# A two-block transformer kernel on one core: inputs laid out for the first stage, weight slabs split in two steps, eight buffers for convolution taps

## The chip, the core and the metric

The kernel runs on one core of a Trainium2 chip. Times are device microseconds of one execution. Engines: PE (TensorE) multiplies matrices, DVE (VectorE) and ACT (ScalarE) work elementwise, POOL (GpSimd) does elementwise work beside them, and SP's queue issues most of the loads. Everything is float32 in memory; the large matrix products run on float32r operands.

## The reference, cut to what matters

Two transformer blocks over 512 positions of 1024 channels, batch 1. The first stage, where most of the change lies, computes this:

```
cond  = silu(c) @ ada_w + ada_b            # six vectors of 1024
h     = rmsnorm(x, norm1_g) * (1 + scale1) + shift1
z     = h @ w_in + b_in                    # u, v, val, gate: 512 columns each
y_a   = gelu(u) * (causal w_s applied to layernorm(gelu(v)) in chunks of 128 positions)
y     = val * sigmoid(gate)
y_b   = silu(groupnorm(causal depthwise convolution of y, width 31))
x     = x + gate1 * (concat(rmsnorm(y_a), rmsnorm(y_b)) @ w_out)
```

A gated feed-forward layer, a final modulated norm, and a second block (two kinds of attention, two feed-forward layers, a pooling mixer) follow. Their program text is not touched.

## The kernel before, in words

Activations lie with channels on the 128 partitions: X holds eight tiles of 128 channels by 512 positions, two to a buffer. A product keeps float32 accuracy by splitting each operand into a high and a low part: `wh`, `wl` for weights, two halves of `H` for activations, and three matmuls for each pair (wh by high, wh by low, wl by high).

Weights come in slabs of 128 by 1024 elements (512 KB) in the order of a list. `Weights.load` (lines 296 to 318) starts a slab's load on SP's queue; the closure `split` (line 312) copies it to `wh` on ACT and subtracts to get `wl` on DVE. `take` hands out the oldest split slab and then splits further ones until `look` (4) are ready, so both halves of a split stand at the same place of the program. The slabs of `w_in` and `w_out` carry a raised priority (`HP`, line 50).

Which engine runs which instruction when is set by a scheduler at build time that goes by priorities and its own estimates, except where `ordered(True)` (lines 557 to 851) pins the order on DVE, ACT and PE to that of the program. Buffers are recycled by tag; "ar" tiles of 4 KB a partition hold slabs, adaptive-norm weights and most other large tiles.

The first stage goes as follows (lines 232 to 851). Small vectors are loaded as rows and turned by PE (`load_vecs`, `turn`). x arrives by positions, four loads; ACT sums its squares, PE turns it by 32 transposes, and DVE copies the result to X. The weights of shift1 and scale1 arrive as sixteen loads of 512 KB; one `piece(q)` takes four of them, computes 256 columns of each vector in sixteen float32 matmuls on four column groups of PE, adds up the groups, and gives `front(q)` what it needs to make two tiles of H. `products(q)` then multiplies these two tiles with the first four slabs of `w_in`, 24 matmuls into four PSUM banks ("wave"), which stay open over q = 0 to 3. In each q but the last, the next piece's matmuls are put after 6 products (`WV`), its transposes after 4 more (`WT`).

After the wave, `glu_out` makes the convolution's input, and `conv` puts 31 taps for each of four channel tiles into two work lists: the first `nd` (23, then 17) taps run on DVE as one multiply-add each into PSUM, the rest as a scaled copy on ACT into a `tap` buffer (line 748, two buffers) and an add on POOL. `pump` deals these lists out between the products of the other twelve slabs of `w_in` and the first of `w_out`. `center` needs both sums complete. The causal spatial weights are loaded as `wsr`, masked on POOL, turned by eight PE transposes (lines 904 to 908) and copied to `wsT` by ACT.

The functions that the diff touches and their callers:

Of the kernel before, what the change touches and what calls it, by code (L numbers as in the profile page):

```python
# [9 lines left out]
F32 = mybir.dt.float32  # L10
# [15 lines left out]
WV = (6, 0)  # L26
WT = 4
DEEP = 2
# [55 lines left out]

TAGS = {}
TAGSETS = 0
B1 = ("cv", "glu", "bvs", "wsr", "wsT", "vt", "uT")
NB1 = 11
# [32 lines left out]
def body(ctx: ExitStack, tc: tile.TileContext, I: dict, out, dbg=None):  # L121
# [7 lines left out]
    V, G, SC, TE = (Ordered(tc, e) for e in (nc.vector, nc.gpsimd, nc.scalar, nc.tensor))  # L129
# [78 lines left out]
    def flat(apx):  # L208
        n = len(apx.shape)
        letters = "abcde"[:n]  # L210
        return apx.rearrange(f"{' '.join(letters)} -> ({' '.join(letters)})") if n > 1 else apx

    def load_vecs(gi, grp, eng=nc.sync):

        rt = rows.rearrange("p a (s c) -> p (a s) c", c=P)[:, gi]
        r0 = 0
        for name, src, n in grp:
            eng.dma_start(rt[r0:r0 + n, :P], flat(src).rearrange("(r p) -> r p", p=P))
            r0 += n

        def turn():
            pt = ST()
            TE.transpose(pt[:, :r0], rt[:r0, :P], ident[:r0, :r0])
            col = C(r0)
            V.tensor_copy(col, pt[:, :r0])
            c0 = 0
            for name, src, n in grp:
                vecs[name] = col[:, c0:c0 + n]
                c0 += n
        return turn  # L230

    rows = A("rows")
    turn_c = load_vecs(0, [("c", I["c"], 8)])
    xt = []
    for i in range(4):
        a = A("xtok")
        nc.sync.dma_start(a, I["x"][0, i * P:(i + 1) * P, :].rearrange("p (j c) -> p j c", j=2))
        xt.append(a)
    turn_1 = load_vecs(1, [("norm1", I["norm1_g"], 8), ("adab", I["ada_b"], 48), ("b_in", I["b_in"], 16)], nc.scalar)
# [36 lines left out]
    Xp = [cp.tile([P, 2, S], F32, name=f"X{q}") for q in range(4)]  # L276

    def x_(k, c0=0, c1=S):
        return Xp[k // 2][:, k % 2, c0:c1]

# [3 lines left out]
    class Weights:  # L284


        def __init__(self, look):
            self.look, self.deep = look, 1
            self.specs, self.loaded, self.ready, self.done = [], [], [], 0
            self.pool = False  # L290
            self.hp = 0
# [4 lines left out]
        def load(self):  # L296
            parts, kt, ncols, pool, hp = self.specs[self.done]
            n = kt * ncols

            def fl(t):  # L300
                return t.rearrange("p a c -> p (a c)")[:, :n]

            def v(t):
                return fl(t).rearrange("p (k m) -> p k m", k=kt)

            raw = ar.tile([P, 2, S], F32, tag="raw", name="raw", bufs=NR) if NR else A("raw")
            for (p0, p1, c0, c1, src, *ks) in parts:
                k0, k1 = ks or (0, kt)
                nc.sync.dma_start(v(raw)[p0:p1, k0:k1, c0:c1], src)
# [8 lines left out]
            self.loaded.append(split)  # L318

        def _emit(self):  # L320
            while len(self.loaded) < self.deep and self.done < len(self.specs):
                self.load()
            self.loaded.pop(0)()
# [228 lines left out]
    turn_2 = load_vecs(2, [("cw", I["b_conv_w"], 124)])  # L552
    turn_3 = load_vecs(3, [("norm2", I["norm2_g"], 8), ("normf", I["norm_f_g"], 8), ("conv_b", I["b_conv_b"], 4), ("gn_g", I["b_gn_g"], 4),
                           ("gn_b", I["b_gn_b"], 4), ("ona", I["out_norm_a_g"], 4), ("onb", I["out_norm_b_g"], 4), ("lng", I["a_ln_g"], 4),
                           ("lnb", I["a_ln_b"], 4), ("psc", I["pool_scale_2"], 8), ("adafb", I["ada_f_b"], 16), ("pe", I["nsa_cmp_pe_2"], 32)])

    ordered(True)
    turn_c()
    act(cact, vecs["c"], AF.Silu)
    V.tensor_copy(c32, cact.unsqueeze(2).to_broadcast([P, KD, 32]))  # L560
    ssx = C(8).rearrange("p (a b) -> p a b", a=4)
    rsc = C(4)
    for i in range(4):
        for j in range(2):
            act(SQ(), xt[i][:, j], AF.Square, accum_out=ssx[:, i, j:j + 1])
    V.tensor_reduce(rsc, ssx, axis=AX.X, op=OP.add)
    act(rsc, rsc, AF.Sqrt, scale=1.0 / D, bias=epsc)
    V.reciprocal(rsc, rsc)
    for k in range(KD):
        pt = AXP()  # L570
        for i in range(4):
            TE.transpose(pt[:, i * P:(i + 1) * P], xt[i][:, k // 4, (k % 4) * P:(k % 4 + 1) * P], ident)
        V.tensor_copy(x_(k), pt)
    rsx = ACC()
    act(rsx, spread(rsc, S), AF.Copy)
    W.ahead(2)
    turn_1()
    adab = vecs["adab"]

    def piece(q):  # L580

        g = [ada_cols(adaw[q][x], 8 * x + 2 * q, adab[:, 8 * x + 2 * q:8 * x + 2 * q + 2], AXP) for x in range(2)]
        for x in g:
            for _ in range(8):
                yield next(x)
        for x in g:
            yield from x
# [128 lines left out]
    def conv(cs, c0, c1, nd):  # L716
# [119 lines left out]
    for q in range(4):  # L836
        w = products(q)
        if q < 3:
            pc = piece(q + 1)
            for n in WV:  # L840
                for _ in range(n):
                    next(w)
                for _ in range(8):
                    next(pc)
# [8 lines left out]
    turn_2()  # L853
    turn_3()
# [49 lines left out]
    for b in range(2):  # L904
        pt = ST()
        for h in range(4):
            TE.transpose(pt[:, h * P:(h + 1) * P], wsr[:, b, h * P:(h + 1) * P], ident)
        act(wsT[:, b], pt, AF.Copy)
    turn_4()
# [324 lines left out]
    W.deep = DEEPF  # L1234
    f1 = Ffn(HO)
# [553 lines left out]

# [16 lines left out]
```

## Time and profile before

| | us |
|---|---|
| median of 3 runs | 1663.76 |
| lowest and highest run | 1662.12, 1664.29 |
| the profiled execution | 1662.05 |
| its span, first to last instruction | 1660.3 |
| PE busy in it | 1626.7 (98%) |
| DVE busy | 879.6 (53%) |
| ACT busy | 681.0 (41%) |
| POOL busy | 129.3 (8%) |

Busy time of PE is a union of overlapping matmuls, so a busy PE may still run slowly, at half clock for instance. All matmuls of the program carry the line of one helper, L113, so tiles tell them apart: `mm` is a product's bank, `ax` and `st` are other banks, `xtok` is x by positions, `adaw` are weights of the adaptive norm, `fixed` are small vectors.

### The profile page before, as it was taken

To read this page: it belongs to the slowest core of one execution; us is meant where nothing else is said; L and a number is where in the kernel's file an instruction comes from. 1 tells how busy PE (TensorE), PEld (TensorE's weight loads), DVE (VectorE), ACT (ScalarE), POOL (GpSimd) and SP (SyncE) were. 2 spreads that over 40 slices of the span, in tenths; PEclk is the share of its full clock that TensorE was granted. 3 is DMA by queue.
4 is the path that set the end of the run, shared out by engine and by line. 5 is a ranking of instruction groups with operands and counts; after the bars stand their busy time and mean duration, and the time that the engine had idled before them with its cause. 6 is when DMAs were issued, how large, how long until landed. Compare 5 with 4: busy or idle time off the path is not lost.

```text
span 1660.3 us, 21934 instructions
## 1 busy us (share of the span) xinstructions
PE 1626.7 (98%) x8733; PEld 1355.0 (82%) x8733; DVE 879.6 (53%) x1644; ACT 681.0 (41%) x1231; POOL 129.3 (8%) x144
## 2 busy tenths in 40 slices
PE   7998999999999999999999999999998999999998
PEld 5886698888888998777778888888888998888886
DVE  4799583444433584778857344423257734432244
ACT  4585352322123455455658223313237823322232
POOL 0452000000000011101011000000022100000002
PEclk9999999999999999999999999999999999999999
DMA  9635434445452333301144133234221533232511
GB/s 306 180 113 209 161 99 117 136 132 173 146 139 80 95 79 79 90 26 52 39 134 108 51 101 89 83 107 140 77 89 54 138 89 102 75 108 92 144 38 51
DMA packets 245167, 179.53 MB, mean 108 GB/s; under 512 B 20688, under 2 KB 220224, under 8 KB 245064
## 3 DMA queue, kind: packets, MB, share of 16 engines
q1 hardware_dynamic: 240520, 176.99, 36.2%
q10 hardware_dynamic: 4544, 1.14, 0.4%
q8 instruction: 68, 1.11, 0.3%
q14 instruction: 35, 0.29, 0.1%
HBM read 175.99 MB, written 2.11 MB: 107 GB/s over the span
## 4 chain that ended last, share of the span: by engine, by line
PE 86%; DVE 4%; ACT 1%; issue 0%; DMA 0%; DVEq 0%; ACTq 0%
PE mm L113 80%; PE ax L113 3%; PE st L113 3%; DVE pw L113 1%; ACT sq L113 0%; DMA raw<-in_ffn_w_gate_dram 0%; DVE wl L113 0%; ACT pw L113 0%; DVE XT L113 0%; DVE H L113 0%; DVE sq L113 0%; DVE mg L113 0%; DVE pt L113 0%; DVE lg L113 0%; DVE fk L113 0%
## 5 line engine op out<-in xcount | busy, mean ns | idle before, releaser
L113 PE MATMUL mm<-H,wh 128*128 128x512 f32 (+1 forms) x3168 | 869.8, 360 | 7.4 <-ACT H L113 2.4
L113 PEld LDWEIGHTS mm<-H,wh 128*128 128x128 f32 x3168 | 563.7, 189 | 106.6 <-issue 8.7
L113 PE MATMUL mm<-H,wl 128*128 128x512 f32 (+1 forms) x1584 | 567.9, 359 | 0.0
L113 DVE TENSOR_TENSOR wl<-raw,wh 128x1024 fp32r<-128x1024 f32 (+1 forms) x257 | 309.7, 1218 | 232.9 <-ACT wh L113 219.8
L113 PEld LDWEIGHTS mm<-H,wl 128*128 128x128 f32 x1584 | 299.3, 189 | 46.8 <-issue 3.4
L113 ACT ACTIVATE wh<-raw 128x1024 fp32r<-128x1024 f32 (+1 forms) x257 | 261.4, 1040 | 132.6 <-PE mm L113 66.6
L113 PE MATMUL mm<-wh,hid 128*128 128x512 f32 x704 | 217.4, 389 | 0.0
L113 DVE TENSOR_TENSOR silu<-silu,mm 128x512 f32<-128x512 f32 (+1 forms) x77 | 47.0, 611 | 252.2 <-PE mm L113 248.2
L113 PEld LDWEIGHTS mm<-wh,hid 128*128 128x128 f32 x704 | 132.1, 188 | 27.1
L113 ACT ACTIVATE hid<-silu 128x512 fp32r<-128x512 f32 (+1 forms) x77 | 43.9, 570 | 254.7 <-DVE silu L113 254.7
L113 PE MATMUL mm<-wl,hid 128*128 128x512 f32 x352 | 137.3, 390 | 0.0
L113 PE MATMUL mm<-hid,wh 128*128 128x512 f32 (+1 forms) x464 | 117.1, 341 | 0.0
L113 PEld LDWEIGHTS mm<-hid,wh 128*128 128x128 f32 x464 | 80.2, 190 | 10.7 <-issue 1.2
L113 POOL TENSOR_TENSOR mg<-mg,gb 128x512 f32<-128x512 f32 x32 | 44.2, 1388 | 464.7 <-ACT sq L113 459.1
L113 ACT ACTIVATE silu<-silu 128x512 f32<-128x512 f32 (+1 forms) x52 | 29.3, 565 | 124.7 <-DVE silu L113 124.7
L113 PE MATMUL mm<-hid,wl 128*128 128x512 f32 (+1 forms) x232 | 79.0, 341 | 0.0
L113 PEld LDWEIGHTS mm<-wl,hid 128*128 128x128 f32 x352 | 66.1, 188 | 14.1 <-DVE wl L113 0.3
L113 DVE TENSOR_TENSOR silu<-mm,rsb 128x512 f32<-128x512 f32 (+1 forms) x52 | 31.6, 608 | 73.3 <-PE mm L113 72.6
L113 PE MATMUL mm<-wh,H 128*128 128x512 f32 (+2 forms) x256 | 66.0, 345 | 2.8 <-ACT wh L113 1.6
L113 DVE TENSOR_TENSOR hid<-silu,hid 128x512 fp32r<-128x512 f32 (+1 forms) x77 | 47.3, 614 | 32.5 <-ACT hid L113 32.5
L113 POOL TENSOR_TENSOR cv<-cv,tap 128x488 f32<-128x488 f32 (+12 forms) x40 | 52.5, 1345 | 88.1 <-ACT cv L113 71.1
L113 DVE SCALAR_TENSOR_TENSOR ax<-glu,fixed,ax 128x511 f32<-128x511 f32 (+21 forms) x76 | 51.4, 732 | 0.0
(271 smaller groups left out, 1582.8 us busy)
## 6 DMA issues: line engine op xcount, KB each, us to landing
adaw<-in_ada_w_dram SPq DMA_DIRECT2D x48, 512.0 KB
raw<-in_w_ffn_in_dram SPq DMA_DIRECT2D x44, 512.0 KB
raw<-in_ffn_w_gate_dram SPq DMA_DIRECT2D x44, 512.0 KB
raw<-in_ffn_w_up_dram SPq DMA_DIRECT2D x44, 512.0 KB
raw<-in_ffn_w_down_dram SPq DMA_DIRECT2D x44, 512.0 KB
raw<-in_w_in_dram SPq DMA_DIRECT2D x16, 512.0 KB
adaw<-in_ada_f_w_dram SPq DMA_DIRECT2D x16, 512.0 KB
raw<-in_attn_w_in_dram SPq DMA_DIRECT2D x16, 512.0 KB
```

Of the source, the lines that this page charges most:

```text
L113: ins = f(*a, **k)
```

## The change

Host-side layout: a function `laid_out` permutes (no arithmetic) some inputs before the one launch: all small vectors into two arrays with channels on partitions (`va`, `vb`), x transposed (`xt`), the shift1 and scale1 weights cut by piece (`ada_p`), `w_in` cut into slabs (`w_in_p`), the spatial weights transposed (`wst`). Every such load then reads 4 KB in a row for each partition where slabs of `w_in` read 512 bytes and `adaw` 1 KB at a time. The turns of vectors, x and spatial weights leave the program, and with them the copies that took their results out of PSUM.

Order of loads: x, the first piece's weights, four slabs of `w_in`, the other pieces' weights, `vb`, in this order on SP. Sums of squares are taken by channel tiles (eight ACT squares, seven DVE adds) and closed on PE. A piece is 32 matmuls of 128 columns, one transpose and two adds. `warm(n)` issues n float32 matmuls of 512 columns whose result nobody reads. `products` goes by part (wh by high, wh by low, wl by high), then by slab.

Slabs: `split` becomes a generator with the `wh` copy ahead of its `yield` and the `wl` subtraction behind it. From the end of the wave until the feed-forward layer, `early` is set and `look` is 3: each `ahead` finishes splits until three are ready and then runs the first half of the next.

Taps: `tap` has eight buffers.

```diff
-WV = (6, 0)
+WV = (16, 8, 8)
 WT = 4
+WM = (7, 1, 2)
...
-B1 = ("cv", "glu", "bvs", "wsr", "wsT", "vt", "uT")
-NB1 = 11
+B1 = ("cv", "glu", "bvs", "wsT", "vt", "uT")
+NB1 = 10
...
+    load_vecs("va", VA, nc.scalar)
+    SY.on = True
+    for q in range(4):
+        SY.dma_start(Xp[q], I["xt"][q])
...
             def split():
+
                 wh, wl = A("wh", F32R), A("wl", F32R)
                 with tc.high_priority(offset=hp) if hp else nullcontext():
                     act(fl(wh), fl(raw), AF.Copy)
+                yield
+                with tc.high_priority(offset=hp) if hp else nullcontext():
                     (G if pool else V).tensor_tensor(fl(wl), fl(raw), fl(wh).bitcast(F32), op=OP.subtract)
                 self.ready.append((v(wh), v(wl), kt))
...
+        def head(self):
+
+            while len(self.loaded) < max(self.deep, 1) and self.done < len(self.specs):
+                self.load()
+            if self.loaded and not self.headed:
+                next(self.loaded[0])
+                self.headed = True
...
         def ahead(self, n):
             while (self.done < len(self.specs) or self.loaded) and len(self.ready) < n:
-                self._emit()
+                self.emit()
+            if self.early:
+                self.head()
...
     adaw = []
     for q in range(4):
-        if q < 2:
-            W.load()
-            W.load()
-        adaw.append([ada_load(ada, c0 + HS * q, HS) for c0 in (0, D)])
...
+        sl = [A("adaw") for _ in range(4)]
+        for a, src in zip(sl, I["ada_p"][q]):
+            SY.dma_start(a, src)
+        adaw.append(sl)
+        if q == 0:
+            for _ in range(4):
+                W.load()
+    SY.on = False
+    load_vecs("vb", VB, nc.sync)
...
+        for _ in range(n):
+            TE.matmul(wb[0], lhsT=ident, rhs=ones[:, 0:1].to_broadcast([P, S]), start=True, stop=True)
+    accx0 = ACC()
     for k in range(KD):
+        acc_sq(accx0, k == 0, x_(k), 0, S)
...
+        pq = AXP()
+        for k in range(KD):
+            for j in range(4):
+                yield TE.matmul(pq[32 * j:32 * j + 32, :P], lhsT=c32[:, k, :], rhs=adaw[q][k // 2][:, k % 2, j * P:(j + 1) * P],
+                                start=(k == 0), stop=(k == KD - 1))
+        sb = T("adasb")
+        act(sb[:, :P], pq[:, :P], AF.Copy)
         pt = AXP()
...
+        yield TE.transpose(pt[:, :P], sb[:, :P], ident)
+        for x in range(2):
+            ks = slice(8 * x + 2 * q, 8 * x + 2 * q + 2)
+            tt(mod[:, ks], pt[:, :P].rearrange("p (j r) -> p j r", j=4)[:, 2 * x:2 * x + 2, 0], adab[:, ks], OP.add)
...
+    warm(WM[0])
     pc = piece(0)
+    for _ in range(8):
+        next(pc)
+    warm(WM[1])
+    for _ in range(8):
+        next(pc)
+    rs0 = rstd(accx0, 0, S, D)
+    for _ in range(8):
+        next(pc)
+    rsp = spread(rs0, S)
+    for _ in range(9):
+        next(pc)
+    W.head()
     drain(pc)
-    front(0)
+    warm(WM[2])
+    front(0, rsp)
+    W.ahead(2)
...
-                t = tp.tile([P, S], F32, tag="tap", name="tap", bufs=2)[:, :c1 - b]
+                t = tp.tile([P, S], F32, tag="tap", name="tap", bufs=8)[:, :c1 - b]
...
     def products(q):
-        for h in ((0, 1), (2, 3)):
-            for k in (2 * q, 2 * q + 1):
-                for x in h:
-                    wh, wl, _ = sl[x]
-                    yield from hx.mm3s(wave[x], k, wh[:, k], wl[:, k], 0, S, k == 0, k == 7)
+        for part in range(3):
+            for x in range(4):
+                for k in (2 * q, 2 * q + 1):
+                    yield TE.matmul(wave[x], lhsT=sl[x][part // 2][:, k], rhs=hx.t[k][:, part % 2, :], start=(part == 0 and k == 0),
+                                    stop=(part == 2 and k == 7))
...
+            for _ in range(WV[q]):
+                next(w)
+            for _ in range(32):
+                next(pc)
             for _ in range(WT):
                 next(w)
             drain(pc)
-            front(q + 1)
+            front(q + 1, rsp)
         drain(w)
+    W.look = 3
+    W.early = True
     W.ahead(3)
     ordered(False)
...
+    nc.sync.dma_start(wsT, I["wst"])
+    G.affine_select(wsT, wsT, pattern=[[0, 8], [1, P]], compare_op=OP.is_ge, fill=0.0, base=0, channel_multiplier=-1)
...
     W.deep = DEEPF
+    W.look = 4
+    W.early = False
     f1 = Ffn(HO)
```

## Rows read from the trace of the kernel before

**Rows 1.** Busy time by stage: stretch, its us, each engine's busy us, clock, DMA, GB/s.
```profile
0.00:23.49 23.49, 11.95 (x78) 8.94 (x78) 11.26 (x31) 12.31 (x27) 1.32 (x11) 0.98 0.96 295
23.49:55.81 32.32, 32.32 (x204) 22.81 (x205) 16.42 (x33) 12.85 (x19) 0.00 (x0) 0.91 0.86 254
55.81:124.50 68.69, 68.69 (x346) 55.84 (x344) 64.01 (x95) 52.20 (x82) 44.53 (x36) 1.00 0.46 142
124.50:175.00 50.50, 46.20 (x301) 29.37 (x298) 45.01 (x62) 25.87 (x38) 9.05 (x7) 1.00 0.65 240
```
**Rows 2.** Timeline to the second piece: start, us, engine, operation, [idle before, releaser].
```profile
19.50 0.64 PE L113 MATMUL ax<-adaw,fixed 128*32 128x256 f32 x8 [0.79 <-DMA adaw<-in_ada_w_dram]
...
20.71 0.44 PE L113 MATMUL st<-fixed,adasb 128*128 128x128 f32 x2 [0.20 <-ACT adasb L113]
...
21.93 1.41 DVE L113 SCALAR_TENSOR_TENSOR t<-X,fixed,acc 128x512 f32<-128x512 f32 x2
22.72 1.39 ACT L113 ACTIVATE H<-t,fixed 128x512 fp32r<-128x512 f32 x2 [2.07 <-DVE t L113]
...
23.49 1.58 PE L113 MATMUL mm<-H,wh 128*128 128x512 f32 x2 [2.35 <-ACT H L113]
24.01 1.98 ACT L113 ACTIVATE wh<-raw 128x1024 fp32r<-128x1024 f32 x2
...
26.71 3.29 PE L113 MATMUL ax<-adaw,fixed 128*32 128x256 f32 x32
```
**Rows 3.** Stretches of 1 us (columns as in rows 1).
```profile
2.00:3.00 1.00, 0.24 (x1) 0.17 (x1) 0.41 (x2) 0.78 (x1) 0.06 (x2) 1.00 0.70 222
...
26.00:27.00 1.00, 1.00 (x6) 0.26 (x9) 1.00 (x2) 0.00 (x0) 0.00 (x0) 0.50 1.09 348
...
29.00:30.00 1.00, 1.00 (x17) 0.42 (x9) 0.00 (x0) 0.16 (x1) 0.00 (x0) 0.75 1.07 342
```
**Rows 4.** Two stretches with saturated DMA engines (columns as in rows 1).
```profile
19.50:38.00 18.50, 15.95 (x111) 9.50 (x111) 11.05 (x23) 6.55 (x12) 0.00 (x0) 0.82 1.10 340
...
165.00:172.00 7.00, 7.00 (x37) 3.66 (x36) 3.77 (x5) 1.26 (x2) 0.00 (x0) 1.00 1.03 410
```
**Rows 5.** Timeline of SP's queue, first loads and the fifth slab.
```profile
4.82 7.71 SPq L249 DMA_DIRECT2D adaw<-in_ada_w_dram  x4
...
44.98 3.02 SPq L309 DMA_DIRECT2D raw<-in_w_in_dram  x2
```
**Rows 6.** Timeline of PE, a later piece, products alone, and short or small matmuls.
```profile
44.05 1.93 PE L113 MATMUL ax<-adaw,fixed 128*32 128x256 f32 x32
...
86.90 1.52 PE L113 MATMUL mm<-wh,H 128*128 128x512 f32 x6
...
99.83 1.04 PE L113 MATMUL st<-fixed,wsr 128*128 128x128 f32 x8
...
122.64 1.97 PE L113 MATMUL st<-fixed,rs 128*64 128x128 f32 x32
...
165.40 1.88 PE L113 MATMUL st<-cv,fixed 128*128 128x512 f32 x4
```
**Rows 7.** Timeline of DVE around the convolution.
```profile
56.55 1.22 DVE L113 TENSOR_TENSOR wl<-raw,wh 128x1024 fp32r<-128x1024 f32 x1
...
58.51 1.52 DVE L113 TENSOR_SCALAR ax<-glu,fixed 128x512 f32<-128x512 f32 x2
...
62.56 1.43 DVE L113 TENSOR_TENSOR wl<-raw,wh 128x1024 fp32r<-128x1024 f32 x1
...
68.81 1.36 DVE L113 TENSOR_TENSOR wl<-raw,wh 128x1024 fp32r<-128x1024 f32 x1 [0.89 <-ACT wh L113]
...
161.98 1.28 DVE L113 TENSOR_TENSOR cv<-cv,ax 128x512 f32<-128x512 f32 x2
```
**Rows 8.** Waits of ACT and of POOL from 0 to 175 us: us in total, times, longest.
```profile
ACT tap L113 <- POOL cv L113: 2.1, 4, 0.8
...
POOL cv L113 <- ACT tap L113: 17.0, 5, 6.0
```

More of the change, by code (lines that the diff above doesn't have):

```diff
@@ L82 @@
 PS3 = 1
+VA = (("c", 8), ("norm1", 8), ("adab", 48), ("b_in", 16))
+VB = (("cw", 124), ("norm2", 8), ("normf", 8), ("conv_b", 4), ("gn_g", 4), ("gn_b", 4), ("ona", 4), ("onb", 4), ("lng", 4), ("lnb", 4),
+      ("psc", 8), ("adafb", 16), ("pe", 32), ("ng2", 64))
+SOURCE = {"c": "c", "norm1": "norm1_g", "adab": "ada_b", "b_in": "b_in", "cw": "b_conv_w", "norm2": "norm2_g", "normf": "norm_f_g",
+          "conv_b": "b_conv_b", "gn_g": "b_gn_g", "gn_b": "b_gn_b", "ona": "out_norm_a_g", "onb": "out_norm_b_g", "lng": "a_ln_g",
+          "lnb": "a_ln_b", "psc": "pool_scale_2", "adafb": "ada_f_b", "pe": "nsa_cmp_pe_2", "ng2": "norm_g_2"}
 TAGS = {}
 TAGSETS = 0
-B1 = ("cv", "glu", "bvs", "wsr", "wsT", "vt", "uT")
-NB1 = 11
+B1 = ("cv", "glu", "bvs", "wsT", "vt", "uT")
+NB1 = 10
 WW = ()
@@ L127, in body @@
     ps = ctx.enter_context(tc.tile_pool(name="ps", bufs=1, space=PSUM))
-    V, G, SC, TE = (Ordered(tc, e) for e in (nc.vector, nc.gpsimd, nc.scalar, nc.tensor))
+    V, G, SC, TE, SY = (Ordered(tc, e) for e in (nc.vector, nc.gpsimd, nc.scalar, nc.tensor, nc.sync))
     def ordered(on):
@@ L206, in body, with load_vecs, x_ @@
     vecs = {}
[L208 to L239, printed above, removed]
+    def load_vecs(src, names, eng):
+        n = sum(w for _, w in names)
+        col = C(n)
+        eng.dma_start(col, I[src])
+        c0 = 0
+        for name, w in names:
+            vecs[name] = col[:, c0:c0 + w]
+            c0 += w
+    Xp = [cp.tile([P, 2, S], F32, name=f"X{q}") for q in range(4)]
+    def x_(k, c0=0, c1=S):
+        return Xp[k // 2][:, k % 2, c0:c1]
+    load_vecs("va", VA, nc.scalar)
+    SY.on = True
+    for q in range(4):
+        SY.dma_start(Xp[q], I["xt"][q])
     ada = I["ada_w"][0]
@@ L274, in ada_cols @@
         tt(mod[:, col:col + n], rd[:, :n], bias, OP.add)
-    Xp = [cp.tile([P, 2, S], F32, name=f"X{q}") for q in range(4)]
-    def x_(k, c0=0, c1=S):
-        return Xp[k // 2][:, k % 2, c0:c1]
     H = [cp.tile([P, 2, S], F32R, name=f"H{k}") for k in range(KD)]
@@ L290, in __init__ @@
             self.pool = False
+            self.headed = self.early = False
             self.hp = 0
@@ L308, in load @@
                 k0, k1 = ks or (0, kt)
-                nc.sync.dma_start(v(raw)[p0:p1, k0:k1, c0:c1], src)
+                SY.dma_start(v(raw)[p0:p1, k0:k1, c0:c1], src)
             self.done += 1
@@ L315, in split, with emit @@
                     act(fl(wh), fl(raw), AF.Copy)
+                yield
+                with tc.high_priority(offset=hp) if hp else nullcontext():
                     (G if pool else V).tensor_tensor(fl(wl), fl(raw), fl(wh).bitcast(F32), op=OP.subtract)
                 self.ready.append((v(wh), v(wl), kt))
-            self.loaded.append(split)
-        def _emit(self):
+            self.loaded.append(split())
+        def head(self):
[4 more added lines that the diff above has]
+                self.headed = True
+        def emit(self):
             while len(self.loaded) < self.deep and self.done < len(self.specs):
                 self.load()
-            self.loaded.pop(0)()
+            self.headed = False
+            drain(self.loaded.pop(0))
         def ahead(self, n):
             while (self.done < len(self.specs) or self.loaded) and len(self.ready) < n:
-                self._emit()
+                self.emit()
+            if self.early:
+                self.head()
         def take(self):
@@ L347, in body, with plan_win @@
     w_in = I["w_in"][0]
+    def plan_win(c):
+        W.plan([(0, P, 0, P, I["w_in_p"][c].rearrange("p (k m) -> p k m", k=8))], 8, P)
     for c in range(4):
@@ L350, in body @@
         W.hp = HP
-        plan_cols(w_in, 0, 8, 1024 + c * P, P)
-        plan_cols(w_in, 0, 8, 1536 + c * P, P)
+        plan_win(8 + c)
+        plan_win(12 + c)
     for b in range(4):
@@ L355, in body @@
     for c in range(4):
-        plan_cols(w_in, 0, 8, c * P, P)
+        plan_win(c)
     for k0 in (0, 4):
@@ L557, in body @@
+        for a, src in zip(sl, I["ada_p"][q]):
[6 more added lines that the diff above has]
+    load_vecs("vb", VB, nc.sync)
     ordered(True)
-    turn_c()
     act(cact, vecs["c"], AF.Silu)
     V.tensor_copy(c32, cact.unsqueeze(2).to_broadcast([P, KD, 32]))
[L561 to L565, printed above, removed]
@@ L566, in body, with warm @@
-    V.tensor_reduce(rsc, ssx, axis=AX.X, op=OP.add)
-    act(rsc, rsc, AF.Sqrt, scale=1.0 / D, bias=epsc)
-    V.reciprocal(rsc, rsc)
-    for k in range(KD):
[L570 to L577, printed above, removed]
+    wb = [None]
+    def warm(n):
+        if wb[0] is None:
+            wb[0] = MM()
+        for _ in range(n):
+            TE.matmul(wb[0], lhsT=ident, rhs=ones[:, 0:1].to_broadcast([P, S]), start=True, stop=True)
@@ L578, in body @@
+    accx0 = ACC()
+    for k in range(KD):
+        acc_sq(accx0, k == 0, x_(k), 0, S)
     adab = vecs["adab"]
     def piece(q):
[L582 to L587, printed above, removed]
+        pq = AXP()
[5 more added lines that the diff above has]
+        act(sb[:, :P], pq[:, :P], AF.Copy)
+        pt = AXP()
+        yield TE.transpose(pt[:, :P], sb[:, :P], ident)
+        for x in range(2):
+            ks = slice(8 * x + 2 * q, 8 * x + 2 * q + 2)
+            tt(mod[:, ks], pt[:, :P].rearrange("p (j r) -> p j r", j=4)[:, 2 * x:2 * x + 2, 0], adab[:, ks], OP.add)
@@ L589, in body, with front @@
     g1 = C(KD)
     hx = HO
-    def front(q):
+    def front(q, rs):
         ks = slice(2 * q, 2 * q + 2)
@@ L598, in front @@
                 t = ts_[k] = T()
-                stt(t, x_(k), g1[:, k:k + 1], rsx, OP.mult, OP.mult)
+                stt(t, x_(k), g1[:, k:k + 1], rs, OP.mult, OP.mult)
                 act(hx.t[k][:, 0], t, AF.Identity, bias=mod[:, k:k + 1])
@@ L839, in body @@
             pc = piece(q + 1)
[L840 to L844, printed above, removed]
+            for _ in range(WV[q]):
+                next(w)
+            for _ in range(32):
+                next(pc)
             for _ in range(WT):
@@ L852, in body @@
     bin_ = vecs["b_in"]
-    turn_2()
-    turn_3()
     cw = vecs["cw"].rearrange("p (t c) -> p t c", c=4)
@@ L902, in body @@
     tt(nmu, nmu, vrs, OP.mult)
[L904 to L909, printed above, removed]
     pr = ST()
@@ L1787, with laid_out @@
 _OUT = (1, 512, 1024)
+def laid_out(a):
+    import numpy as np
+    a = {k: np.asarray(v) for k, v in a.items()}
+    for name, group in (("va", VA), ("vb", VB)):
+        a[name] = np.concatenate([a[SOURCE[v]].reshape(w, P).T for v, w in group], axis=1)
+    a["xt"] = a["x"][0].T.reshape(4, 2, P, S).transpose(0, 2, 1, 3)
+    p = a["ada_w"][0][:, :2 * D].reshape(4, 2, P, 2, 4, 2, P)
+    a["ada_p"] = p.transpose(4, 0, 2, 1, 3, 5, 6).reshape(4, 4, P, 2, S)
+    a["w_in_p"] = a["w_in"][0].reshape(KD, P, 16, P).transpose(2, 1, 0, 3).reshape(16, P, D)
+    a["wst"] = a["a_spatial_w"][0].transpose(2, 0, 1).reshape(P, 2, S)
+    return a
 def kernel(**inputs):
@@ L1796 @@
     arrays, args = {}, {}
-    for name, a in inputs.items():
+    for name, a in laid_out(inputs).items():
         a = np.ascontiguousarray(a)
```

8 lines of the change are left out of this document (removed).

## The prediction, made before the change was run

> **What bounds the kernel now.** I read the page's slices first: PE is busy in nine tenths or more of nearly every slice, so a change to another engine counts only where PE waits or runs slowly. Busy time by stage [rows 1] shows where that is. Up to 23.49 us, when the first product of `w_in` starts, PE is busy 11.95 us; to the wave's end at 55.81 it is always busy, but at a mean clock of 0.91; then it streams without a gap, while DVE has 64.0 us of work in 68.7; from 124.5 to 175 it idles 50.5 - 46.2 = 4.3 us, with DVE busy 45.0 us. What comes after 175 us is not edited.
>
> The timeline of the opening [rows 2] says what holds the first product: loads. The last eight matmuls of piece 0 wait 0.79 us for `adaw` and start at 19.50; copies and transposes end at 20.71 + 0.44 = 21.15; then adds, `t` on DVE at 21.93, `H` on ACT at 22.72, product at 23.49. The 32 transposes of x had ended before that wait, so dropping them alone is worth nothing. The idle 2.35 us ahead of 23.49 is followed by a granted clock of 0.50, 1.2 GHz, which is back only within the slice from 29 us [rows 3]. In that stretch a piece's 32 records take 3.29 us, later 1.93 [rows 2, 6].
>
> **The change part by part.** Times are those of the profiled execution: 1662.05 us with its span of 1660.3; the three runs have their median at 1663.76, 1.7 higher, and I carry the difference over to it.
>
> *Loads.* Bytes flow from about 2 us [rows 3]. Before, x (four loads of 0.524 MB), piece 0 (four) and two slabs queued among them make 5.24 MB by 19.5 us. Now x and piece 0 come first, 4.19 MB. The nearest rows for the rate are 340 GB/s with 1 KB rows of the same weights and 410 with 4 KB rows [rows 4]; all loads are now of the second kind, and I take 400 as the start is ragged. Issue does not hold them: `adaw` by 1 KB rows cost SP 7.71 us for four [rows 5], and longer rows mean fewer pieces to issue. Then x is in at 2.2 + 5.2 = 7.4, piece 0 at 12.7, four slabs at 17.9, the other pieces at 23.1, 28.4 and 33.6 us. At 340 GB/s the first two are 8.4 and 14.5, the last 39.2.
>
> The Trainium skill, "DMA: Bandwidth & Descriptors", section "Where 436 GB/s comes from", says that reads from HBM are held by about 358 GB/s per core, whatever the fabric could do. By it x and piece 0 would be in at about 13.9 (an estimate from that page), and the gain below 1.2 us smaller. The measured 410 over 7 us [rows 4] is above that limit, so the sum keeps the row.
>
> *First product.* Squares (eight ACT, seven DVE, about 0.65 us each) keep up with x. PE has seven idle-filling matmuls at 1.88/2 = 0.94 us [rows 6], done at about 8.5 us, before the first slab of piece 0. From 12.7: last eight matmuls 0.6 (eight records of twice the width took 0.64), evacuation 0.4, one transpose 0.3: 14.3 us. From there to the first product it took 23.49 - 21.15 = 2.3; two reductions go, 2.0 stays: 16.3 instead of 23.5, a gain of 7.2. The two `warm` matmuls there cover 1.9 us of that gap, so I keep the clock at full. If PE ran the opening at half clock, the first seven would take 13 us and the first product come 2 to 3 us later.
>
> *The wave.* PE's work is 96 products at 0.227 us (six in 1.52 us less an overlap of 0.16 [rows 6]) = 21.8 us, and three pieces. A piece of 16 matmuls in 32 records took 1.93 us; now it has 64 records of half the width on four column groups. If width decides, it stays 1.93; if each record costs what the nearest narrow ones do, 1.97/32 = 0.062 us [rows 6], it is 3.9. Those rows run on two groups, not four, so I take 2.6, plus 0.15 for one transpose instead of 0.35 for four: 21.8 + 8.3 = 30.1 us. Waits come on top. ACT must make `H` twice (0.7 each) and `wh` of slabs 2 to 4 (1.0 each [rows 2]) while PE needs only 1.8 us for part one: about 1.6 us. Piece 1 has landed at 23.1, about 0.7 us after PE has done sixteen products. Four products (0.9) and twelve or four more cover the 3 us chain of `front`; behind piece 1 only four are left, so about 1.0 + 0.5 is open. Wave end: 16.3 + 30.1 + 3.8 = 50.2, against 55.81: a gain of 5.6 us. It was 7.2 at the start and 3.1 from the restored clock; 4.7 is paid back in waits and smaller records.
>
> *Between wave and convolution.* DVE's taps start at 58.51 [rows 7], 2.7 us behind the wave's end, with one `wl` (1.22) and a vector copy among it; `wl` of the sixth and seventh slab stands at 56.55 and 62.56 because SP starts the fifth slab's load only at 44.98 [rows 5], behind thirteen small vector loads. These are now one load, so both subtractions fit into DVE's idle half of the wave [rows 1]. But part order ends all four banks within the last 0.9 us, where two banks used to end 2.7 us early. Taps start at about 50.2 + 1.6 = 51.8: 6.7 us earlier, and 1.4 more for the second `wl`.
>
> *Head of a split.* DVE waits for ACT's `wh` twice after the wave, 0.89 at 68.81 [rows 7] and 0.4 at 104: with `wh` one take ahead 1.3 us goes at best. No instruction is added, and the load goes out as early as with `look` 4.
>
> *Taps.* Two buffers make ACT wait 2.1 us for POOL in all, and POOL waits 17.0 us for ACT [rows 8]. Neither is on the path: POOL is busy 9 of 50 us in the last stretch [rows 1], and `center` of the second convolution comes at 161.98 [rows 7] behind DVE's own taps. Zero, from -1 to +1.5: with POOL adding, `wl` took 1.43 instead of 1.22 [rows 7], so seven splits moved under POOL's adds cost 1.5 us. The Trainium skill, "GPSIMD Engine Reference", section "1. Specifications", has GpSimd's SBUF interface shared with VectorE, in contention with two-input instructions; the two rows agree, and it speaks against packing POOL's adds together. The sum stays as it is, since their number does.
>
> *Turns.* PE loses the eight records of `wsr` and a turn, about 1.2 us [rows 6], DVE three vector copies (0.8), ACT two copies.
>
> *Sum.* At the end of the wave 5.6. To 124 us PE's side is 5.6 + 1.2 = 6.8 and DVE's is 6.7 + 1.4 + 1.3 + 0.2 = 9.6. The last stretch is where PE waits for DVE, so up to 2.8 of its idle 4.3 us goes; I take half of that: 6.8 + 1.4 = 8.2, call it 8.0, as the scheduler redoes its order of later work and small losses are as likely as gains. Profile 1654.0; median of runs 1655.8. Bounds: with 340 GB/s, pieces at 3.9 and nothing from DVE the gain is 8.2 - 1.9 - 3.9 - 1.4 = 1; with pieces at 1.93, 410 GB/s, no waits of ACT and all idle time gone it is 8.2 + 2.0 + 0.3 + 1.6 + 2.9 = 15.
>
> **Rivals.** *The gain is lost again before 175 us.* DVE's 45.0 of 50.5 us busy says that the last stretch belongs to it; if its taps don't start earlier (late `wl`, late banks, ACT busy with taps that eight buffers let it run ahead on), only the turns and the head are left, about 2 us: 1661.8. Against it: nothing that DVE needs is tied to a fixed time.
>
> *Half clock through the wave.* The idle 2.35 us before 23.49 was followed by 1.2 GHz for some 7 us at about 3 us of cost. Now PE pauses between slabs of piece 0 and in part one; if the clock stays at 0.50 while the wave lasts, 30 us of work cost some 25 more: 1655.8 + 25 = 1681. It turns into a loss from about 16 us at half clock. Against it: it came back in six.
>
> *Slabs come late, slower than before.* With three split slabs and not four, `wl` is issued one take later, on DVE, which has hardly a gap. Twelve takes of `w_in` follow the wave; if PE waited behind one tap and one `wl` (0.7 + 1.2 us) at most of them, 15 us would go: 1655.8 + 15 = 1671. It decides from 0.7 us a take on. Against it: three slabs are 16 us of products.
>
> *All of PE's idle time goes too.* DVE's lead of 2.8 us plus the faster pieces: 1650.5.
>
> **How the numbers follow.** Forecast 0.69 with 1652 to 1659.5 as its own range; everything better 0.10; gain lost 0.13; half clock 0.03; late slabs 0.05. The range, 1649.5 to 1661.0, leaves half of the third out, most of the last two and the end of the second. A measurement tells 0.2%, 3.3 us, from no change: faster than 1660.4 has 0.69 + 0.10 + 0.01 = 0.80, same 0.12, slower 0.03 + 0.05 = 0.08.
>
> **What would show it.** The first product at 15.5 to 18.5 us; no 0.50 in the clock from there on; x, piece 0 and slabs at about 400 GB/s; a piece in 1.9 to 3.9 us; wave end at 48.5 to 52; first DVE tap near 52; PE idle under 3 us between 115 and 170; the feed-forward layers as long as before. I am wrong if the first product is early and the 175 us mark is not, if DVE waits for `wh` as often as before, or if PE waits for `wl` after the wave.

## The result: slower by 0.62%, and the profile after

Six runs of the changed kernel have a median of 1673.71 us (1672.78 to 1674.43), six of the kernel before beside them 1663.53 (1662.12 to 1664.29): a ratio of 1.0062, 95% interval 1.0052 to 1.0073. The profiled execution took 1673.59 us with a span of 1671.9. The forecast was 1655.8, range 1649.5 to 1661.0: wrong in size and in sign.

The opening went much as forecast. Busy time by stage after the change, beside [rows 1] (columns as there; the first boundary is again the first product, the second the wave's end):

```profile
0.00:18.73 18.73, 16.48 (x101) 8.04 (x101) 8.02 (x23) 9.41 (x16) 1.27 (x11) 1.00 0.91 357
18.73:51.64 32.91, 30.59 (x293) 22.95 (x293) 18.14 (x30) 12.34 (x18) 0.00 (x0) 1.00 0.92 332
51.64:120.00 68.36, 56.06 (x246) 44.88 (x245) 51.16 (x71) 41.97 (x67) 44.84 (x38) 0.92 0.16 54
120.00:170.00 50.00, 46.87 (x326) 34.34 (x326) 43.52 (x65) 34.10 (x49) 8.00 (x5) 0.97 0.56 187
```

The first product comes 4.8 us earlier, the wave ends at 51.64 in place of 55.81, and the clock is 1.00 throughout. The loss is in the third row. PE, busy all the time there before, is busy 56.06 of 68.36 us, at a clock of 0.92. PE's timeline shows one wait that makes most of it:

```profile
108.82 0.39 PE L120 MATMUL mm<-H,wh 128*128 128x512 f32 x1
119.24 3.75 PE L120 MATMUL st<-cv,fixed 128*128 128x512 f32 x4 [10.04 <-DVE cv L120]
```

PE stands 10.04 us for `center` of the first convolution, and the four records behind the wait take 3.75 us, where the same four took 1.88 at full clock [rows 6]. So DVE is late. Its timeline from 97 us:

```profile
97.30 1.36 DVE L120 SCALAR_TENSOR_TENSOR ax<-glu,fixed,ax 128x493 f32<-128x493 f32 x2
101.45 2.06 DVE L120 TENSOR_TENSOR wl<-raw,wh 128x1024 fp32r<-128x1024 f32 x1 [2.79 <-POOL cv L120]
...
105.31 1.99 DVE L120 SCALAR_TENSOR_TENSOR ax<-glu,fixed,ax 128x491 f32<-128x491 f32 x3
114.50 2.05 DVE L120 TENSOR_TENSOR wl<-raw,wh 128x1024 fp32r<-128x1024 f32 x1 [7.20 <-POOL cv L120]
...
118.42 1.27 DVE L120 TENSOR_TENSOR cv<-cv,ax 128x512 f32<-128x512 f32 x2
```

`wl` is `raw` minus `wh`; POOL makes neither. A wait of `wl` for POOL's `cv<-cv,tap` can only be for the place that `wl` is written to: a tap lay there that POOL had not yet added. POOL's timeline beside it, and ACT's, which makes the taps:

```profile
74.08 0.15 POOL L120 MEMSET cv<- 128x17 f32 x2
92.71 25.90 POOL L120 TENSOR_TENSOR cv<-cv,tap 128x494 f32<-128x494 f32 x21 [18.48 <-ACT cv L120]
```

```profile
74.00 0.71 ACT L120 ACTIVATE tap<-glu,fixed 128x494 f32<-128x494 f32 x1 [2.35 <-DVE glu L120]
...
83.41 1.31 ACT L120 ACTIVATE tap<-glu,fixed 128x494 f32<-128x494 f32 x2 [6.23 <-DVE glu L120]
84.62 1.04 ACT L120 ACTIVATE wh<-raw 128x1024 fp32r<-128x1024 f32 x1
85.57 3.08 ACT L120 ACTIVATE tap<-glu,fixed 128x493 f32<-128x493 f32 x5
...
91.94 1.29 ACT L120 ACTIVATE cv<-glu,fixed 128x495 f32<-128x495 f32 x2
```

With eight buffers ACT has made eight taps of the second convolution by 88.7 us, but POOL may not add the first before `cv` is begun at 91.94. From 92.71 it adds 21 in 25.90 us without a pause. In the compiled placement the first late `wl` lies on the fourth and seventh tap added, and the second late one on the eighteenth. POOL's seventh and eighteenth addition, seen by themselves:

```profile
100.16 1.25 POOL L120 TENSOR_TENSOR cv<-cv,tap 128x492 f32<-128x492 f32 x1
113.43 1.04 POOL L120 TENSOR_TENSOR cv<-cv,tap 128x486 f32<-128x486 f32 x1
```

They end at 101.41 and 114.47; the late `wl` start at 101.45 and 114.50.

DVE's waits for splits from 44 to 180 us (total, times, longest), beside 1.5 us for `wh` and none for POOL before:

```profile
DVE wl L120 <- POOL cv L120: 10.0, 2, 7.2
DVE wl L120 <- ACT wh L120: 5.9, 3, 3.5
```

**A ledger.** The first feed-forward product of DVE's marks the end of all edited work: 229.9 us before, 240.0 after.

```profile
L113 DVE TENSOR_TENSOR silu<-silu,mm x77: 411/687/689, 229.9 to 1620.3; 128x512 f32<-128x512 f32 x55, 128x256 f32<-128x256 f32 x22
```

```profile
L120 DVE TENSOR_TENSOR silu<-silu,mm x77: 412/687/689, 240.0 to 1631.8; 128x512 f32<-128x512 f32 x55, 128x256 f32<-128x256 f32 x22
```

The whole 10 us is there by then. For each kernel I add, over stretches of 4 us from 44 to 240 us, PE's idle time and its busy time times (1 - granted clock). Before: 5.2 idle, 0.0 clock. After: 16.0 and 3.4. That is 14.2 us more of PE's time; the marker is only 10.1 later, so 4.1 us of the edits' gain are still in it.

### The profile page after: what moved, and what is told of

It is laid out like the page before. It is cut to its first block, busy times and chain, and to the rows that moved or that the text cites. A ratio compares the mean times of both kernels' runs of the same rounds, so it can differ in the third digit from the quotient of the medians.

```text
span 1671.9 us, 22075 instructions
## 1 busy us (share of the span) xinstructions
PE 1634.5 (98%) x8832; PEld 1355.5 (81%) x8832; DVE 877.4 (52%) x1629; ACT 678.5 (41%) x1216; POOL 127.3 (8%) x144
## 4 chain that ended last, share of the span: by engine, by line
PE 86%; DVE 3%; ACT 2%; issue 0%; DVEq 0%; ACTq 0%
PE mm L120 79%; PE ax L120 4%; PE st L120 3%; DVE pw L120 1%; ACT sq L120 0%; ACT pw L120 0%; DVE wl L120 0%; DVE XT L120 0%; ACT H L120 0%; DVE sq L120 0%; DVE pt L120 0%; DVE lg L120 0%; DVE fk L120 0%; DVE mg L120 0%; DVE sd L120 0%
## 5 line engine op out<-in xcount | busy, mean ns | idle before, releaser
L120 PE MATMUL mm<-hid,wh 128*128 128x512 f32 (+1 forms) x464 | 117.0, 341 | 0.0
L120 PEld LDWEIGHTS mm<-wh,H 128*128 128x128 f32 x256 | 44.9, 193 | 8.4 <-ACT wh L120 3.2
```

The lines of the kernel that those rows point to most:

```text
L120: ins = f(*a, **k)
```

## The experiments

All are compared with the kernel before in runs on the same chip. "POOL" and "ACT" are DVE's waits of `wl` for POOL's `cv` and ACT's `wh` between 44 and 180 us; "center" is the first `cv<-cv,ax`; "PE" is the ledger's idle + clock; "FFN" is its marker. The last five columns come from one profiled execution of each kernel, and executions of one kernel lie up to 8.2 us apart (a_pin12), so small differences in these columns say little.

| kernel | us | ratio to before, 95% | POOL | ACT | center | PE | FFN |
|---|---|---|---|---|---|---|---|
| before | 1662 to 1664 | 1 | 0 | 1.5 | 106.9 | 5.2 | 229.9 |
| changed | 1673.7 | 1.0062 (1.0052-1.0073) | 10.0 | 5.9 | 118.4 | 19.4 | 240.0 |
| a_tap2 | 1665.1 | 1.0017 (1.0007-1.0026) | 0 | 8.8 | 109.5 | 11.1 | 231.4 |
| a_look4 | 1670.7 | 1.0045 (1.0030-1.0060) | 10.0 | 5.9 | 117.9 | 19.6 | 238.0 |
| a_first | 1672.2 | 1.0056 (1.0039-1.0072) | 0 | 8.9 | 109.2 | 16.5 | 237.3 |
| b_tap8 | 1670.7 | 1.0048 (1.0033-1.0063) | 0 | 10.0 | 117.0 | 10.2 | 237.3 |
| b_early | 1665.6 | 1.0012 (1.0003-1.0022) | 0 | 1.5 | 105.7 | 5.8 | 230.3 |
| a_pin8 | 1660.7 | 0.9986 (0.9977-0.9996) | 0 | 4.2 | 107.5 | 9.3 | 228.2 |
| a_tap4 | 1669.9 | 1.0039 (1.0025-1.0053) | 5.5 | 5.9 | 114.4 | 17.5 | 237.1 |
| a_pool | 1665.3 | 1.0012 (1.0003-1.0022) | 0 | 8.8 | 109.4 | 17.1 | 233.8 |
| b_pin8 | 1665.1 | 1.0018 (1.0009-1.0028) | 0 | 7.3 | 112.1 | 5.2 | 232.1 |
| a_first_pin8 | 1662.7 | 1.0005 (0.9996-1.0014) | 0 | 4.2 | 108.7 | 13.2 | 232.3 |
| a_pin8_nd21 | 1670.3 | 1.0049 (1.0037-1.0062) | 0 | 10.5 | 105.7 | 18.6 | 236.4 |
| b_pin8_nd21 | 1672.6 | 1.0065 (1.0052-1.0079) | 0 | 12.4 | 111.4 | 13.2 | 238.9 |
| a_pin4 | 1665.3 | 1.0015 (1.0005-1.0025) | 0 | 8.5 | 109.0 | 10.1 | 230.5 |
| a_pin12 | 1667.8 | 1.0026 (1.0014-1.0039) | 0 | 4.3 | 107.3 | 16.6 | 235.4 |
| a_pin8_nd24 | 1665.7 | 1.0018 (1.0008-1.0027) | 0 | 4.8 | 109.9 | 17.1 | 233.5 |
| a_pin8_nd25 | 1668.8 | 1.0038 (1.0024-1.0052) | 0 | 4.8 | 111.2 | 17.5 | 236.5 |

**The parts one by one.** a_tap2 takes the taps' buffers back, a_look4 the split's head, a_first both; b_tap8 and b_early put one part alone into the kernel before.

```
a_tap2, a_first: -  name="tap", bufs=8)   +  name="tap", bufs=2)
b_tap8:          -  name="tap", bufs=2)   +  name="tap", bufs=8)
a_look4, a_first (and its counterpart ahead of f1):
-    W.look = 3
-    W.early = True
b_early: the two lines, split() in two steps and head()
```

a_tap2: 

> The changed kernel with two tap buffers in place of eight; nothing else is undone. Theory T (the eight buffers): they are taken from the memory in which weight slabs lie, and they let ScalarE run far ahead of GpSimd with taps, so a slab's low part waits for GpSimd's additions (10.0 us of VectorE in 44-180 us of the changed kernel) and its high part stands behind waiting taps (5.9 us). Then this kernel has neither: first centring of the convolution near 102 us in place of 118.4, and 1655 to 1660 us, below before (1663.5). Rival H (the head split one take ahead): the taps are bystanders, so 1670 to 1675 as with eight. Rival F (the first stage, that moves everything 5 us up and repacks the memory): also 1670 to 1675.

Measured 1665.1, above T's range and below those of H and F: the waits for POOL are gone and 8.6 us with them. T's first half holds; but center came at 109.5, not 102, and the waits for `wh` grew to 8.8 us, so its second half fell.

a_look4: 

> The changed kernel with four slabs ahead and no head split early, as before; eight tap buffers stay. Theory T (the eight buffers): the waits for GpSimd stay, 1668 to 1676 us, centring still after 113 us. Rival H (the head split early): the loss goes, 1655 to 1660 us. Rival F (the first stage): 1670 to 1675 us.

Measured 1670.7, both waits as in the changed kernel to 0.1 us. H falls; T and F both allow this time.

a_first: 

> The laid-out first stage alone: two tap buffers, four slabs ahead, no early head. Theory T and rival H: the 4 to 5 us that the first stage gained reach the end, 1656 to 1661 us; by T it is within 3 us of the kernel with two tap buffers. Rival F: 1670 to 1675 us.

Measured 1672.2: a miss for T and H, and inside the range of F, which a_tap2 had not met. Neither eight buffers nor the split's head is in this kernel, and the faster opening alone is 9.5 us slower than before. DVE waits 8.9 us for `wh`, but it waits 8.8 us in a_tap2 too, which is 7.1 us faster; PE stands here:

```profile
109.90 1.98 PE L120 MATMUL st<-cv,fixed 128*128 128x512 f32 x4 [2.84 <-DVE cv L120]
...
144.72 0.50 PE L120 MATMUL mm<-H,wh 128*128 128x512 f32 x1 [2.98 <-DVE H L120]
146.16 0.80 PE L120 MATMUL mm<-H,wh 128*128 128x512 f32 x1 [0.48 <-DVE H L120]
```

The record at 146.16 takes 0.80 in place of 0.50: after the waits of 2.98 and 0.48 us the clock is low again, 0.50 from 146.1 to 149 us.

b_tap8: 

> The kernel before with eight tap buffers and nothing else. Theory T: the waits appear here too, first centring at 115 to 124 us in place of 106.9, 1672 to 1682 us (before 1663.5 and some 12 us). Rival H and rival F: within 3 us of 1663.5.

Measured 1670.7, 1.3 below T's range, center at 117.0: eight buffers cost 8 us without the rest of the change. But T's wait isn't there: `wl` waits 10.0 us for `wh` and never for POOL, and in this kernel's compiled placement no slab lies on a tap. What shows instead is ACT's queue. Taps stand in it waiting for POOL, `wsT` behind them, and PE's longest wait between 44 and 180 us is for `wsT`:

```profile
107.03 0.70 ACT L113 ACTIVATE tap<-glu,fixed 128x488 f32<-128x488 f32 x1 [2.13 <-POOL cv L113]
109.23 0.70 ACT L113 ACTIVATE tap<-glu,fixed 128x488 f32<-128x488 f32 x1 [1.49 <-POOL cv L113]
110.23 0.70 ACT L113 ACTIVATE tap<-glu,fixed 128x487 f32<-128x487 f32 x1 [0.31 <-POOL cv L113]
110.84 1.06 ACT L113 ACTIVATE wsT<-st 128x512 f32<-128x512 f32 x2
```

```profile
PE st L113 <- ACT wsT L113: 5.2, 1, 5.2
```

b_early: 

> The kernel before with the head of a split taken one slab ahead and three slabs ahead, nothing else. In the changed kernel, taking these two away while two tap buffers are kept costs 7 us more (1672.2 against 1665.1), with both traces alike up to 110 us. Theory E (fewer slabs in flight free memory for loads, so the edit gains by itself): 1656 to 1661 us. Rival N (the edit does nothing by itself, its worth depends on the planner's order in each kernel): within 2 us of before, 1661 to 1665. Rival H (it delays slabs): 1666 us or more.

Measured 1665.6, +0.12%: N, 0.6 us above its range. The head's worth has no sign of its own: on top of a_first 7.1 us are gained (to a_tap2), of a_look4 3.0 lost (to the changed kernel), of a_first_pin8 2.0 gained.

**Whose memory.** Eight buffers in a place that no slab uses (the last line as the later runs write it):

```
+    pins = [cp.tile([P, S], F32, name=f"tap{n}") for n in range(8)]
...
-                t = tp.tile([P, S], F32, tag="tap", name="tap", bufs=8)[:, :c1 - b]
+                t = pin()[:, :c1 - b]
```

a_pin8: 

> The changed kernel with its eight tap buffers put in 16 KB of their own per partition, that no slab ever uses; ScalarE may run as far ahead as with eight. Theory M (the loss is shared memory: a slab written where a tap lay must wait for GpSimd's addition): VectorE's waits of a slab's low part for GpSimd (10.0 us) vanish and those for its high part (5.9 us) stay; first centring 106 to 110 us in place of 118.4, 1660 to 1668 us. Rival Q (the loss is ScalarE's queue, in which a high part stands behind taps that wait for GpSimd): the loss stays, centring after 115 us, 1670 us or more. Both allow for the 16 KB missing later, which could add some us after 250 us.

Measured 1660.7 us, 13 below the changed kernel. It is the one version whose median lies below both kernels, though by 0.14% only, less than the 0.2% that I called no change. ACT still runs ahead, POOL still adds 20 taps without a pause; only the place is another:

```profile
89.26 24.75 POOL L120 TENSOR_TENSOR cv<-cv,tap 128x494 f32<-128x494 f32 x20 [13.91 <-ACT cv L120]
```

```profile
97.28 1.77 DVE L120 TENSOR_TENSOR wl<-raw,wh 128x1024 fp32r<-128x1024 f32 x1 [2.08 <-ACT wh L120]
...
104.09 1.32 DVE L120 TENSOR_TENSOR wl<-raw,wh 128x1024 fp32r<-128x1024 f32 x1 [1.25 <-ACT wh L120]
...
107.45 1.27 DVE L120 TENSOR_TENSOR cv<-cv,ax 128x512 f32<-128x512 f32 x2
```

M holds for the changed kernel, but for the waits for `wh`, which went from 5.9 to 4.2 us in place of staying; Q falls. The pair with four buffers, shared and their own (`range(4)`), and the kernel before with eight of its own:

a_tap4: 

> The changed kernel with four tap buffers. Theory M (shared memory): four buffers touch fewer slab places than eight, so a time between the kernel with two (1665.1) and with eight (1673.7): 1666 to 1671 us, with a VectorE wait for GpSimd of 1 to 6 us. Rival Q (ScalarE's queue): four leave as little waiting as eight and the loss is that of eight within 2 us.

Measured 1669.9 with a wait for POOL of 5.5 us: M, and 3.8 us below eight, where Q allowed 2.

a_pin4: 

> The changed kernel with four tap buffers in 8 KB of their own. Theory M: beside four shared ones (1669.9) the VectorE wait for GpSimd (5.5 us) goes and the high part's wait stays, so 1660 to 1665 us, close to eight of their own (1660.7). Rival: it was the number eight and not the place that helped, 1667 us or more.

b_pin8: 

> The kernel before with eight tap buffers in 16 KB of their own. Theory M (shared memory makes the loss of the eight): the 8 us that eight shared buffers cost here (1670.7) go, 1660 to 1665 us, no VectorE wait of a low part for GpSimd between 44 and 180 us. Rival Q (ScalarE running ahead makes it): 1668 us or more. A rival that 16 KB less for slabs costs by itself would show as a time above 1665 without such waits.

a_pin4 and b_pin8 end 0.3 and 0.1 us above M's ranges. With four the place is worth 4.6 us (1669.9 to 1665.3), and the wait for POOL of 5.5 us goes with it, while the waits for `wh` grow from 5.9 to 8.5. In the kernel before, 5.5 of the 8 us come back, as M said, but not by M's mechanism: b_tap8 has no slab on a tap and no wait of `wl` for POOL that could go. PE's wait for `wsT` is 1.0 us here in place of 5.2; which part of the new placement put ACT's work into another order is not shown, and neither is whether 16 KB less for other tiles cost the last 0.1 us. So in the changed kernel the buffers' memory is the cause of the waits for POOL, shown with eight and with four; in the kernel before, eight buffers cost 8 us too, and the trace points to ACT's queue, which no edit tested alone.

**What eats the rest of the lead.** In a_pool the first two `cv` of ACT and the first two taps keep program order, and POOL's mask comes after its first 14 additions:

```
+            ins = act(y_(c)[:, b - c0:], glu[c][:, b - nd:c1 - nd], AF.Copy, ...)
+            if cs[0] == 0:
+                keep(ins)
```

a_pool: 

> The changed kernel with two tap buffers, in which the first two scaled inputs of the convolution that GpSimd sums and the first two taps keep their place in ScalarE's program order, and GpSimd's triangular mask comes after its first 14 additions; by the order of the instructions the high parts of four slabs now stand ahead of the taps that wait for GpSimd. Theory Q2 (what eats the first stage's lead with two buffers is the 8 us in which VectorE waits for a high part behind such taps between 50 and 110 us): that wait falls below 3 us, first centring moves from 109.5 to 102 to 105 us, and the time is 1656 to 1662 us. Rival P (GpSimd's own 14 additions bound the convolution): they now begin 10 us or more later, so centring comes later than 109.5 and the time is above 1665.

Measured 1665.3, the wait for `wh` 8.8 and center 109.4 as in a_tap2. Q2 as I built it fell; P's time came, its later center did not. The order was changed, not the waiting.

a_first_pin8: 

> The changed kernel with eight tap buffers of their own, but four slabs ahead and no early head: the first stage and free taps. Theory L (the split's head taken early, with three slabs ahead, is worth some 7 us on top of this first stage, as with two shared buffers: 1672.2 against 1665.1): 1666 to 1671 us. Rival N (that difference was the planner's order in one kernel and not the edit's own worth; in the kernel before it gave nothing): within 3 us of 1660.7.

Measured 1662.7, N: with eight buffers of their own the opening alone is level with before, 9.5 us better than a_first. A wait for a place can't be the reason here: `wl` in a_first never waits for POOL, and both the number and the order of ACT's work changed (its waits for `wh` are 4.2 us in place of 8.9).

Taps moved between DVE and POOL (`ND0 = 23` to 21, 24, 25):

a_pin8_nd21: 

> The changed kernel with eight tap buffers of their own and four of VectorE's taps of the first convolution given to GpSimd (21 in place of 23 lags). Theory B (after the memory wait is gone, the first stage's lead is eaten because VectorE's convolution ends last: TensorE stood 3.3 us for its centring, with a lower clock behind that): 4 taps of 0.66 us leave VectorE, GpSimd has room between 75 and 89 us; centring at 103 to 106 us in place of 107.5, TensorE's wait for it below 1.5 us, 1656 to 1660 us. Rival P (GpSimd's additions end last then): centring not earlier than 107, 1661 us or more.

b_pin8_nd21: 

> The kernel before with the same two edits (eight tap buffers of their own, 21 lags). Theory B: before, TensorE hardly waited for the centring, so this gains little here: 1660 to 1664 us, and the distance to the changed kernel with the same edits is 3 to 5 us, the gain of the first stage with nothing in its way. Rival: the two edits alone bring all of it, and the two kernels lie within 1.5 us.

a_pin8_nd24: 

> Eight buffers of their own and 24 lags on VectorE in the first convolution: two taps fewer for ScalarE and GpSimd, two more of 0.66 us for VectorE. Theory Q3 (21 lags cost 9 us because ScalarE's and GpSimd's chain held the high parts): the high parts come earlier, TensorE's waits for slabs stay at nothing, 1658 to 1662 us. Theory B2 (VectorE's convolution is what ends last and each tap on it counts): 1.3 us later than with 23 and more behind the clock, 1662 to 1665 us.

a_pin8_nd25: 

> As the one before with 25 lags: four taps (2.7 us) more on VectorE, four fewer on GpSimd. Theory Q3: 1657 to 1663 us, high part's wait below 3 us. Theory B2: centring after 109 us, 1663 to 1668 us.

With 21 lags center comes 1.8 us earlier, as B said, and the time is 9.7 us worse: B falls. With four taps more on ACT and POOL, DVE waits 10.5 us for `wh`, and PE now waits for the slabs themselves (PE's waits from 44 to 180 us in a_pin8_nd21):

```profile
PE mm L120 <- DVE wl L120: 4.6, 2, 3.8
PE mm L120 <- ACT wh L120: 2.0, 1, 2.0
PE st L120 <- DVE cv L120: 1.6, 1, 1.6
```

The two kernels with 21 lags lie 2.3 us apart (1670.3, 1672.6), between the two answers; b_pin8_nd21 is 8.6 us above B's range. With 24 and 25 lags center comes later (109.9, 111.2) and the time is 0.7 and 0.8 us above B2's ranges; but the wait for `wh` did not fall (4.8), and with 24 PE's largest wait was one of 5.7 us for an ACT square. B2 has the direction, and its chain is not shown; Q3 falls.

a_pin12: 

> The changed kernel with twelve tap buffers of their own (24 KB). Theory Q3 (what is left of the loss is ScalarE's queue behind GpSimd: VectorE waits 4.2 us for high parts with eight): with twelve, taps wait less, that wait falls below 3 us and the time to 1657 to 1660 us. Rival O (the planner uses the freedom to put more taps ahead of each high part, so the wait is as long): 1660 to 1666 us.

Measured 1667.8, above both ranges, with the wait for `wh` as with eight (4.3). Why it is slower than eight is not shown: twelve also take 8 KB more memory than eight.

## Why the prediction was wrong, step by step

*Loads, first product.* 2.4 us late: 18.73 against 16.3, and just outside the 15.5 to 18.5 given as its sign. (The terms listed, 12.7 + 0.6 + 0.4 + 0.3, make 14.0 and not 14.3.) The rate was right, 398 GB/s from 2 to 18 us against 400, and the last load of piece 0, issued at 4.71, landed 8.8 us later, at 13.5 in place of 12.7:

```profile
2.00:18.00 16.00, 15.60 (x101) 7.58 (x100) 7.21 (x19) 7.93 (x15) 0.01 (x1) 1.00 1.01 398
```

By the Trainium skill, "DMA: Bandwidth & Descriptors", section "Where 436 GB/s comes from", some 358 would have been the limit; the 398 over 16 us decides. The larger part is PE's own queue. Piece 0's last matmuls start at 15.31 without waiting for a load, right behind the matmuls that spread x's norm, which the sum did not have:

```profile
14.22 1.16 PE L120 MATMUL st<-fixed,rs 128*128 128x128 f32 x8
15.31 0.64 PE L120 MATMUL ax<-adaw,fixed 128*32 128x128 f32 x16
```

*The wave.* Its end is 1.4 us off (50.2, measured 51.64), in part by luck: the later start was partly made up by shorter waits of PE, 2.3 us (32.91 - 30.59) in place of 3.8. A piece's 64 records took 1.96 us and not 2.6, so here width decided and not the record:

```profile
24.74 1.96 PE L120 MATMUL ax<-adaw,fixed 128*32 128x128 f32 x64
```

*Between wave and convolution.* DVE's first tap starts at 53.00 (forecast 51.8), 5.5 us earlier than before. I moved all chains by this. POOL's moved by 3.0 only (first the kernel before, then the changed one):

```profile
58.19 1.24 POOL L113 TENSOR_TENSOR cv<-cv,tap 128x488 f32<-128x488 f32 x1 [56.13 <-ACT cv L113]
...
55.14 1.61 POOL L120 TENSOR_TENSOR cv<-cv,tap 128x488 f32<-128x488 f32 x1 [53.13 <-ACT cv L120]
```

Before, POOL started at 58.19, 0.3 us ahead of DVE; now it starts 2.1 behind: between ACT's second `sg` and its first `cv` stood one tap, and now two taps and a `wh`. In a_tap2 `wh` then stands behind taps that wait for POOL, DVE's `wl` waits behind `wh` (8.8 us against 1.5), and the 5.5 us are gone by center (109.5 against 106.9). This is read from the traces; a_pool, the one run that tried to take that wait away, left it at 8.8. Where I priced DVE's side at 9.6 us of gain, center came 2.6 us later even without the eight buffers.

*Head of a split.* Forecast up to 1.3 us better. Alone it is 1.0012 (1.0003 to 1.0022), within what I called no change.

*Taps: "Neither is on the path ... Zero, from -1 to +1.5".* This is the step that failed. I asked whether the waits between ACT and POOL are on the path. I did not ask what else uses the memory that six more buffers take. Measured: two waits of `wl` for POOL, 10.0 us, that go when the buffers have their own place; 13.0 us between eight shared and eight of their own, 8.6 between eight and two. The warning that I did weigh, `wl` under POOL's additions, was the small part: the two late ones took 2.06 and 2.05 us against 1.2 without POOL, about 1.7 us together. The Trainium skill, "GPSIMD Engine Reference", section "1. Specifications", has the two engines' shared SBUF interface in contention when a VectorE instruction has two inputs from SBUF, and these rows agree.

*Sum.* "PE's side is 5.6 + 1.2": the ledger has 4.1 to the marker. The other side was taken as gain or nothing, and cost 14.2 us of PE's time: 8.3 with the eight buffers (19.4 against 11.1 in a_tap2), 5.9 without them. So the taps' step is the largest but not the only one: a_tap2, at 1665.1, is still above the range, because DVE's lead, counted as a gain, didn't reach center.

*Rivals.* The first named the place (lost before 175 us) and even "ACT busy with taps that eight buffers let it run ahead on", but ended at "only the turns and the head are left", 1661.8: it was bounded by the gain, as if a lost lead could not turn into a wait longer than itself. Late slabs, at 1671, came nearest in time, but by another path: with four split slabs again (a_look4) most of the loss stays, and in the changed kernel PE waits only 1.2 us for `wl` and 1.0 for `wh` from 44 to 240 us. Half clock through the wave did not come (1.00); it came after the waits, 3.4 us. All three signs of being wrong came: an early first product with a late marker, DVE waiting for `wh` as often as before (three times, 5.9 us against 1.5), and PE waiting for `wl`.

**What stays open.** In the ledger, FFN less PE's losses is 216 to 221 us (mean 219.0) for the twelve a_ kernels and the changed one, 224 to 227 (mean 225.8) for before and the b_ ones: so the edited opening seems worth some 7 us up to there (each value is of one execution), and what differs most is how PE waits. Why each edit makes other waits (a_first 16.5, a_tap2 11.1, a_pin12 16.6, all with the same opening) I can name wait by wait but not by one cause; the planner (the scheduler at build time) orders every queue anew, and two kernels alike up to 110 us (a_tap2 and a_first) end 7 us apart.

## What to carry to other kernels

Before giving a buffer more copies, ask whose memory they take: here the eight buffers of a lightly used engine became the reason why DVE could not write. A wait whose releaser makes none of the operands may be a wait for a place: look up what lay there. Here it went when the taps got another place. More copies also let a queue run ahead, and work for others then stands behind it, as `wsT` did in b_tap8. Of a lead won at the start, ask what each chain behind it moves up; follow each queue, ACT's with its mixed work above all, and not only the engine that looked bound.

## What was not expected of the hardware

PE pays twice for standing still: after 9.9 us without a record the granted clock was 0.51, 1.2 GHz, for the next 3.8 us, though it had been 1.00 through the opening, when PE never stood as long.

```profile
109.30:119.20 9.90, 0.00 (x0) 0.67 0.21 84
119.20:123.00 3.80, 3.76 (x5) 0.51 0.13 25
```

These two rows show PE's busy time, records, clock, DMA share and GB/s. A wait of 2.85 us did it too (a_tap2, up to 110.22: clock 0.50 from 110 to 115 us).
